# A hybrid retention and attention trunk on one core: score matmuls of one height, projections grouped, output halves sharing their accumulators

## The chip, the cores and the metric

The kernel runs on one core of a Trainium2 chip. The metric is the device time of one execution in microseconds, the median of the runs shown. TensorE (PE; its weight loads are PEld), VectorE (DVE), ScalarE (ACT), GpSimd (POOL) and SyncE (SP) each work through an instruction stream of their own and wait for one another by semaphores.

## The reference, cut to what matters

512 tokens of width 1024 pass through two layers. Each layer is: half a SwiGLU feed-forward, a token mixer, half a SwiGLU feed-forward, a gated extra embedding; an RMS norm stands ahead of each. The mixer of layer 0 is retention (4 heads), that of layer 1 is attention with a forget gate (16 heads of 64), which is where most of the change lies:

```
q, k, v, fz = split(h @ w_in)                         # 16 heads of 64, fz: 16 logits a token
c = cumsum(log_sigmoid(fz + b_f))                     # over the tokens
logits = (q @ k.T) * scale + c[query] - c[key]        # causal
o = softmax(logits) @ v
return o.reshape(S, 1024) @ w_out
```

## The kernel before, in words

Activations are kept with features on the partitions and the 512 tokens along the free dimension (`h[m]`, eight blocks). Each fp32 operand is split into a rounded part (hi) and a rest (lo), and a product is three matmuls (`mm3`, L301 to L303: hi with hi, hi with lo, lo with hi). Weights come through SP's queue into `wraw` (4 buffers); ACT makes the hi part (L79), and DVE or POOL, whichever `W.low` names, the lo part (L80), into `w` (3 buffers). `W.plan` is the order of all weights; `W.take` insists on that order and prepares two ahead. A PSUM accumulator is one of 8 banks (`bank()`). The order on PE is the order of the program text; on the other engines a planner orders the instructions by priority and by estimated times. A norm's scale per token is made in two steps: `n.columns` (L426, then a chain of small DVE and ACT operations) gives it with tokens on partitions, `n.rows` (L445 transposes, L439) spreads it over all partitions. Projections don't need it; their evictions do.

**Retention** (L679) projects q and k of head 0, calls `n.columns` and `n.rows` and spreads the variance (L732 to L734), then projects v (`v_part`, L673 to L675, 96 matmuls). At its end `out_both` (L634) applies the output weights of the last two heads into shared accumulators, four blocks ahead of the last head's results.

**The forgetting attention** (L824) works on pairs of heads, `p` = 0 to 7, with 64 partitions for each head of the pair. First comes the gate: the projection `fz`, columns, rows, and a chain of some thirty DVE and ACT operations on 16 partitions (L835 to L872) to the cumulated gates, which go to DRAM (L873) and come back broadcast, one row for each head (L941), then masked by POOL (L942). `k_part` (L889) and `q_part` (L906) project one pair each (24 matmuls of 512 columns), and split: `khi[e]` holds head e's hi keys on both halves of the partitions, `klo` the lo keys of both heads, each on its own half; `q[e]` holds the hi queries on head e's half and the lo queries on the other. `scores` (L923) then needs two matmuls for each query block i, of (i+1)*128 columns:

```
nc.tensor.matmul(at[i], q[e][own[e], i * P : w], klo[own[e], :w], start=True, stop=False)   # L933: 64 partitions
nc.tensor.matmul(at[i], q[e][:, i * P : w], khi[e][:, :w], start=False, stop=True)          # L936: 128 partitions
```

into three banks for each head, and writes the softmax for DVE and ACT (L955 to L967). `turn` (L972) transposes a head's probabilities (10 transposes, L982, three banks) and splits them (L292, L293); `attend` (L988) multiplies them with v (8 matmuls, L995 and L996) and adds two halves (L998, L999). The order that PE follows in a round of the loop (L1014) is: k projection of pair p+1; attend for head 0 of pair p-1; turn head 0 of pair p; q projection; attend for head 1; turn head 1; scores of pair p+1. Round 0 has no attend and turns both heads after the q projection; round 4 also projects the second half of v (96 matmuls). In round 7 and after, `out_part` (L620) applies the output weights of heads 0 to 7 (96 matmuls in all, each block added to `h[m]`, L630) between the same steps; after the last attend it applies those of heads 8 to 15 (96 matmuls), again with one addition for each block, and prepares the next feed-forward's input block by block (`nxt.block`). `open_ffn(3)` has DVE form weight sums at the same time. The feed-forward that follows starts with `product` (L478), which needs all eight blocks.

Of the kernel before, what the change touches and what calls it, by code (L numbers as in the profile page):

```python
# [17 lines left out]
P = 128  # L18
S = 512
# [154 lines left out]
def trunk(ctx, tc, a):  # L174
# [77 lines left out]
    W.plan += fox_o[0] + fox_o[1]  # L252
# [381 lines left out]
    def out_both(parts, nxt, early, between, late):  # L634


        banks = {}

        def add(i, m, first, last):
            srcs, yhi, ylo = parts[i]  # L640
            j = m % 2
            if (i, m // 2) not in banks:
                banks[i, m // 2] = W.take(srcs[m // 2])
            wh, wl = banks[i, m // 2]
            o = banks.setdefault(m, None)
            if o is None:
                o = banks[m] = bank()
            for k in range(4):
                ks = slice((4 * j + k) * P, (4 * j + k + 1) * P)
                mm3(o, wh[:, ks], wl[:, ks], yhi[k], ylo[k], first and k == 0, last and k == 3)  # L650

        for m in early:
            add(0, m, True, False)
        between()
        for m in early + late:
            if m in late:
                add(0, m, True, False)
            add(1, m, False, True)
            nc.vector.tensor_tensor(out=h[m], in0=banks[m], in1=h[m], op=ALU.add)
            nxt.block(m)  # L660
# [18 lines left out]
    def retention(n, nxt):  # L679
        with ExitStack() as pools:  # L680
            stack = []
            pool = pools.enter_context(tc.tile_pool(name="ret", bufs=1, reuse_waits="tile"))
# [43 lines left out]
            for hd in range(RH):  # L726
                dk = pool.tile([P, S], F32, name="decay", bufs=2)
                nc.sync.dma_start(out=dk, in_=a["decay"][hd])
                if hd == 0:
# [3 lines left out]
                    n.rows()  # L733
                    nc.scalar.mul(epsv, spread(n.v), EPS)  # L734
# [7 lines left out]
                vs = v_part(ret_v[hd], n)  # L742
                v = []
# [71 lines left out]
            def between():  # L815
                outputs()
                pools.close()
                stack.append(open_ffn(1))

            out_both([(ret_o[RH - 2], *before), (ret_o[RH - 1], *y)], nxt, [0, 1, 2, 3], between, [4, 5, 6, 7])  # L820
        return stack[0]


    def forgetting(n, nxt):  # L824
        H = 64
        with tc.tile_pool(name="fox", bufs=1, reuse_waits="tile") as pool:
# [4 lines left out]
            (fz,) = proj([a["fox_f"]], n)  # L831
            n.columns()
            n.rows()
# [54 lines left out]

            def k_part(p):  # L889

                (o,) = proj([fox_qk[p][0]], n)
                t1 = temp()
                nc.vector.tensor_tensor(out=t1, in0=o, in1=n.r, op=ALU.mult)
                klo = pool.tile([P, S], F32R, name="klo")
                khi = []
                for e in range(2):
# [7 lines left out]
                return khi, klo  # L904

            def q_part(p):  # L906

                (o,) = proj([fox_qk[p][1]], n)
# [14 lines left out]
            def scores(p, q, k):  # L923

                khi, klo = k
# [87 lines left out]
            old = None  # L1013
            for p in range(8):  # L1014
                last = p == 7
                if last:
                    out_part(fox_o[0], yhi[0:4], ylo[0:4], None, range(1))
                else:
                    k = k_part(p + 1)
                if old:  # L1020
                    y = temp()
                    attend(p - 1, 0, v, old[0], y)
                    new = [turn(0, sm[0])]
                if last:
                    out_part(fox_o[0], yhi[0:4], ylo[0:4], None, range(1, 2))
                else:
                    q = q_part(p + 1)
# [8 lines left out]
                if not last:  # L1036
                    sm = scores(p + 1, q, k)
# [250 lines left out]
```

## Time and profile before

| | |
|---|---|
| median of 3 runs | 2306.04 us (2305.58 to 2314.34) |
| the profiled execution | 2314.51 us, of which the span is 2312.6 us |
| mean granted TensorE clock | 0.966 of full speed |
| PE busy | 2192.7 us (95%) |
| DVE busy | 1537.3 us (66%) |
| ACT busy, POOL busy | 1210.0 us (52%), 460.0 us (20%) |
| chain that ended last | PE 73%, DVE 10%, ACT 7%, DMA 6% |

The span is read from left to right in 40 slices. Retention fills about 376 to 793 us, the forgetting attention about 1565 to 1864 us, and the feed-forwards the rest. "Idle before" is the time for which an engine stood still ahead of an instruction, with the instruction that ended it.

### The profile page before, as it was taken

The numbers are of one execution on the slowest core, as the hardware profiler recorded it, in microseconds if no ns is written. First come the engines' busy times: TensorE is split into PE (matmuls) and PEld (weight loads), VectorE is DVE, ScalarE is ACT, GpSimd is POOL, SyncE is SP. The second block draws the span as 40 slices with busy tenths as digits, with TensorE's granted clock in tenths as the row PEclk, the third lists the DMA queues.
The fourth block names the chain that finished last, engine by engine and source line by source line (L and its number), as shares of the span: only waits on it lengthen the run. The fifth ranks groups of instructions, "written<-read, shape, count | busy, mean of one in ns | idle before, by whom it ended". The sixth has DMA issues, their size and how long they took to land.

```text
span 2312.6 us, 34447 instructions
## 1 busy us (share of the span) xinstructions
PE 2192.7 (95%) x13417; PEld 1955.9 (85%) x13417; DVE 1537.3 (66%) x2813; ACT 1210.0 (52%) x2022; POOL 460.0 (20%) x347
## 2 busy tenths in 40 slices
PE   7998999999999899999989899999999989999998
PEld 7898987888888798989879899897777779898977
DVE  8676766264453976767687676776775787676774
ACT  7464554333233673646466455455564576363653
POOL 0010103344443010101101011014222211010144
PEclk9999999999999999999999999999889989999998
DMA  6474652222322464646345465543222246464631
GB/s 192 119 179 123 150 143 93 75 96 73 100 82 73 119 163 129 156 131 157 105 127 121 130 150 152 145 115 101 65 64 82 69 108 163 117 160 132 147 109 37
DMA packets 87907, 274.94 MB, mean 119 GB/s; under 512 B 9648, under 2 KB 13232, under 8 KB 87744
## 3 DMA queue, kind: packets, MB, share of 16 engines
q1 hardware_dynamic: 63328, 209.78, 27.7%
q0 software_dynamic: 23184, 61.88, 16.0%
q8 instruction: 105, 1.72, 0.3%
q10 hardware_dynamic: 1232, 1.09, 0.1%
q14 instruction: 58, 0.48, 0.1%
HBM read 270.58 MB, written 2.13 MB: 118 GB/s over the span
## 4 chain that ended last, share of the span: by engine, by line
PE 73%; DVE 10%; ACT 7%; DMA 6%; issue 2%; POOL 0%; SPq 0%; ACTq 0%; DVEq 0%; POOLq 0%
PE bank L478 24%; PE bank L303 13%; PE bank L301 13%; PE bank L302 13%; DMA wraw<-in_ffn_w_in 5%; DVE sums L141 2%; PE bank L673 2%; PE bank L674 2%; PE bank L675 2%; ACT w L117 1%; ACT s L79 1%; DVE w L80 1%; ACT w L118 1%; PE bank L936 1%; PE bank L933 1%
## 5 line engine op out<-in xcount | busy, mean ns | idle before, releaser
L79 ACT CAST w<-wraw 128x1024 fp32r<-128x1024 f32 (+1 forms) x224 | 226.7, 1020 | 443.3 <-PE bank L303 286.4
L80 DVE TENSOR_TENSOR s<-sums,s 128x512 fp32r<-128x512 f32 x344 | 232.6, 687 | 116.0 <-ACT s L79 115.5
L79 ACT CAST s<-sums 128x512 fp32r<-128x512 f32 x344 | 208.2, 617 | 190.4 <-DVE sums L141 139.1
L303 PE MATMUL bank<-unit_a,w 128*128 128x512 f32 (+1 forms) x752 | 292.3, 389 | 4.4 <-DVE w L80 2.7
L301 PE MATMUL bank<-unit_a,w 128*128 128x512 f32 (+1 forms) x752 | 293.4, 390 | 2.4 <-ACT w L79 2.0
L302 PE MATMUL bank<-unit_a,w 128*128 128x512 f32 (+1 forms) x752 | 291.8, 388 | 0.8 <-DVE unit_a L293 0.8
L301 PE MATMUL bank<-unit_d,w 128*128 128x512 f32 (+1 forms) x744 | 287.4, 386 | 3.6 <-ACT w L79 1.8
L302 PE MATMUL bank<-unit_d,w 128*128 128x512 f32 (+1 forms) x744 | 285.6, 384 | 5.1 <-DVE unit_d L296 3.9
L303 PE MATMUL bank<-unit_d,w 128*128 128x512 f32 (+1 forms) x744 | 285.0, 383 | 2.7 <-DVE w L80 2.7
L80 POOL TENSOR_TENSOR w<-wraw,w 128x1024 fp32r<-128x1024 f32 x90 | 220.1, 2449 | 323.5 <-ACT w L79 312.5
L478 PE MATMUL bank<-unit_b,s 128*128 128x256 f32 x952 | 205.1, 282 | 0.0
L119 POOL DMA_DIRECT2D a<-in_ffn_w_in x86 | 75.2, 874 | 612.2 <-ACT a L118 540.3
L478 PE MATMUL bank<-unit_d,s 128*128 128x256 f32 x1188 | 194.3, 281 | 0.0
L119 POOL DMA_DIRECT2D w<-in_ffn_w_in x75 | 65.6, 875 | 645.2 <-ACT w L118 518.2
L478 PE MATMUL bank<-unit_a,s 128*128 128x256 f32 x1314 | 186.6, 279 | 2.9 <-ACT unit_a L361 2.4
L302 PEld LDWEIGHTS bank<-unit_d,w 128*128 128x128 f32 x744 | 145.1, 195 | 32.2 <-DVE unit_d L296 4.1
L141 DVE TENSOR_TENSOR sums<-wraw 128x512 f32<-128x512 f32 x172 | 118.0, 688 | 81.6 <-DMA wraw<-in_ffn_w_in 80.3
L301 PEld LDWEIGHTS bank<-unit_d,w 128*128 128x128 f32 x744 | 145.3, 195 | 31.5 <-ACT w L79 3.5
L478 PE MATMUL bank<-unit_b,w 128*128 128x256 f32 x774 | 147.7, 291 | 25.2 <-ACT tmp L529 24.6
L303 PEld LDWEIGHTS bank<-unit_a,w 128*128 128x128 f32 x752 | 141.5, 188 | 35.5 <-DVE w L80 4.5
L569 DVE SCALAR_TENSOR_TENSOR tmp<-bank,rows 128x512 f32<-128x512 f32 x96 | 66.0, 689 | 158.2 <-PE bank L303 154.5
L478 PEld LDWEIGHTS bank<-unit_a,s 128*128 128x128 f32 x1314 | 167.7, 190 | 3.5 <-ACT unit_a L361 2.6
(266 smaller groups left out, 4942.9 us busy)
## 6 DMA issues: line engine op xcount, KB each, us to landing
wraw<-in_ffn_w_in SPq DMA_DIRECT2D x174, 512.0 KB, 4.6
w<-in_ffn_w_in POOLq DMA_DIRECT2D x75, 512.0 KB, 5.6
wraw<-in_ffn_w_out SPq DMA_DIRECT2D x64, 512.0 KB, 5.0
a<-in_ffn_w_in POOLq DMA_DIRECT2D x86, 256.0 KB, 6.5
wraw<-in_ffn_w_out SPq DMA_DIRECT2D x32, 384.0 KB, 4.3
wraw<-in_ret_qk SPq DMA_DIRECT2D x16, 512.0 KB, 3.4
wraw<-in_ret_v SPq DMA_DIRECT2D x16, 512.0 KB, 3.7
wraw<-in_ret_g SPq DMA_DIRECT2D x16, 512.0 KB, 3.5
```

The costliest lines, as they stand in the source:

```text
L79: self.nc.scalar.copy(hi, raw)
L80: self.low.tensor_tensor(out=lo, in0=raw, in1=hi.bitcast(F32), op=ALU.subtract)
L119: self.nc.gpsimd.dma_start(out=lo, in_=src, accum_op=ALU.add)
L141: add = lambda o, p, q: nc.vector.tensor_tensor(out=o, in0=p, in1=q, op=ALU.add)
L301: nc.tensor.matmul(out, wh, xh, start=first, stop=False)
L302: nc.tensor.matmul(out, wh, xl, start=False, stop=False)
L303: nc.tensor.matmul(out, wl, xh, start=False, stop=last)
L478: add = lambda w, x, start, stop: nc.tensor.matmul(out, w, x, start=start, stop=stop, skip_group_check=True)
L569: nc.vector.scalar_tensor_tensor(out=t1, in0=o, scalar=-0.5, in1=n.r, op0=ALU.mult, op1=ALU.mult)
L673: nc.tensor.matmul(os[t], xh, wh[:, js], start=k == 0, stop=False)
L674: nc.tensor.matmul(os[t], xh, wl[:, js], start=False, stop=False)
L675: nc.tensor.matmul(os[t], xl, wh[:, js], start=False, stop=k == KB - 1)
```

## The change

It has five parts. (1) In retention's head 0 the rows and the variance are spread after `v_part` instead of before it. (2) In the attention the k projection of pair 0 stands ahead of the columns and its q projection ahead of the rows. (3) The lo keys get a tile for each head, `klo0` and `klo1`, zeroed once by POOL on the half that isn't written, so that the L933 matmul can run on all 128 partitions with the same stationary operand as L936. (4) A round is now: k and q projections, both attends, both turns, scores. (5) The output halves share accumulators: `out_both` becomes the class `OutBoth`, used by retention in the same order as before, and by the attention with six blocks of heads 0 to 7 begun ahead of the last attend (two ahead of the attends of round 7, two ahead of its turns, two after them) and the last two blocks at the end; the order of the output weights in the plan follows.

```diff
-    W.plan += fox_o[0] + fox_o[1]
+    W.plan += fox_o[0][0:3] + fox_o[1][0:3] + [fox_o[0][3], fox_o[1][3]]
...
+    class OutBoth:
...
+        def add(self, i, m):
...
+                mm3(self.banks[m], wh[:, ks], wl[:, ks], yhi[k], ylo[k], i == 0 and k == 0, i == 1 and k == 3)
+        def first(self, ms):
+            for m in ms:
+                self.banks[m] = bank()
+                self.add(0, m)
+        def rest(self):
+            for m in range(KB):
+                if m not in self.banks:
+                    self.first([m])
+                self.add(1, m)
+                nc.vector.tensor_tensor(out=h[m], in0=self.banks[m], in1=h[m], op=ALU.add)
+                self.nxt.block(m)
...
     def retention(n, nxt):
...
                     n.columns()
-                    n.rows()
-                    nc.scalar.mul(epsv, spread(n.v), EPS)
...
                 vs = v_part(ret_v[hd], n)
+                if hd == 0:
+                    n.rows()
+                    nc.scalar.mul(epsv, spread(n.v), EPS)
...
     def forgetting(n, nxt):
...
             (fz,) = proj([a["fox_f"]], n)
+            begun = [proj([s], n)[0] for s in fox_qk[0][0:1]]
             n.columns()
+            begun += proj(fox_qk[0][1:2], n)
             n.rows()
...
+            lows = []
+            for e in range(2):
+                lows.append(pool.tile([P, S], F32R, name=f"klo{e}"))
+                nc.gpsimd.memset(lows[e].bitcast(F32), 0.0)
...
-                        out=klo[own[e]], in0=t1[own[e]], in1=kh[own[e]].bitcast(F32), op=ALU.subtract
+                        out=lows[e][own[e]], in0=t1[own[e]], in1=kh[own[e]].bitcast(F32), op=ALU.subtract
...
-                            nc.tensor.matmul(at[i], q[e][own[e], i * P : w], klo[own[e], :w], start=True, stop=False)
+                            nc.tensor.matmul(at[i], q[e][:, i * P : w], lows[e][:, :w], start=True, stop=False)
...
+            both = OutBoth([(fox_o[0], yhi, ylo), (fox_o[1], [], [])], nxt)
             for p in range(8):
-                last = p == 7
-                if last:
-                    out_part(fox_o[0], yhi[0:4], ylo[0:4], None, range(1))
+                if p < 7:
+                    k, q = k_part(p + 1), q_part(p + 1)
                 else:
-                    k = k_part(p + 1)
+                    both.first((0, 1))
                 if old:
                     y = temp()
-                    attend(p - 1, 0, v, old[0], y)
-                    new = [turn(0, sm[0])]
...
+                    for e in range(2):
+                        attend(p - 1, e, v, old[e], y)
                     split_y(y)
...
                 if p == 4:
                     v = v_block(1)
-                new.append(turn(1, sm[1]))
-                if not last:
+                if p == 7:
+                    both.first((2, 3))
+                old = [turn(e, sm[e]) for e in range(2)]
+                if p < 7:
                     sm = scores(p + 1, q, k)
-                old = new
-            out_part(fox_o[0], yhi[0:4], ylo[0:4], None, range(2, 4))
+            both.first((4, 5))
             y = temp()
             for e in range(2):
                 attend(7, e, v, old[e], y)
             split_y(y)
+            both.parts[1] = fox_o[1], yhi[4:8], ylo[4:8]
             W.low = nc.vector
         stack = open_ffn(3)
-        out_part(fox_o[1], yhi[4:8], ylo[4:8], nxt)
+        both.rest()
```

## Rows read from the trace of the kernel before

**Rows 1.** The page: the granted TensorE clock in the span's 40 slices, in tenths.

```profile
PEclk9999999999999999999999999999889989999998
```

**Rows 2.** Busy time by stretch: stretch, length, then PE, PEld, DVE, ACT and POOL busy with their instructions, the granted clock, DMA share, GB/s. The first is from the first score matmul of pair 1 to that of pair 7.

```profile
1629.16:1802.07 172.91, 165.12 (x697) 128.42 (x697) 119.87 (x412) 96.98 (x212) 46.68 (x29) 0.86 0.21 67
1656.00:1682.00 26.00, 24.69 (x100) 18.93 (x100) 19.06 (x67) 14.54 (x33) 5.84 (x5) 0.80 0.20 61
1755.02:1775.72 20.70, 20.60 (x101) 16.27 (x100) 17.60 (x69) 15.17 (x37) 7.20 (x5) 1.00 0.22 76
```

**Rows 3.** The timeline of PE where a round's scores begin and where the next round begins: start, duration, line, operation, tiles, shapes, count, and in brackets the idle time before.

```profile
1657.74 0.62 PE L936 MATMUL bank<-khi,q 128*128 128x256 f32 x2 [1.31 <-DVE q L917]
...
1663.74 0.63 PE L301 MATMUL bank<-unit_d,w 128*128 128x512 f32 x1
1664.17 0.63 PE L302 MATMUL bank<-unit_d,w 128*128 128x512 f32 x1
```

**Rows 4.** The timeline of PE at full clock: scores of one pair without a wait, to the projection after them; one head's turn and the projection after it; two attends in a row, first matmul and the one after the last. The last row is of the attend's line: count, and shortest, median and longest weight load in ns.

```profile
1755.02 0.62 PE L933 MATMUL bank<-klo,q 64*128 64x256 f32 x2
...
1759.85 0.39 PE L301 MATMUL bank<-unit_d,w 128*128 128x512 f32 x1
...
1646.62 1.28 PE L982 MATMUL bank<-ident,p 128*128 128x128 f32 x10
1647.66 0.47 PE L301 MATMUL bank<-unit_d,w 128*128 128x512 f32 x1
...
1837.47 0.40 PE L995 MATMUL bank<-thi,unit_b 128*128 128x512 f32 x1
...
1839.96 0.45 PE L301 MATMUL bank<-unit_a,w 128*128 128x512 f32 x1
...
L995 PEld LDWEIGHTS bank<-thi,unit_b x64: 186/188/193, 1645.2 to 1839.7; 128*128 128x128 f32 x64
```

**Rows 5.** The timeline of PE: round 0 from its two turns on, and the first scores of pair 7.

```profile
1626.62 2.35 PE L982 MATMUL bank<-ident,p 128*128 128x128 f32 x20
1629.16 0.61 PE L933 MATMUL bank<-klo,q 64*128 64x256 f32 x2 [0.19 <-ACT q L916]
1630.95 0.62 PE L936 MATMUL bank<-khi,q 128*128 128x256 f32 x2 [1.19 <-DVE q L917]
1632.39 0.47 PE L933 MATMUL bank<-klo,q 64*128 64x128 f32 x1 [0.82 <-DVE tlo L293]
...
1802.07 0.61 PE L933 MATMUL bank<-klo,q 64*128 64x256 f32 x2 [0.15 <-ACT q L916]
```

**Rows 6.** The timeline of DVE around the scores of the same round as in rows 3.

```profile
1655.80 2.60 DVE L917 TENSOR_TENSOR q<-tmp,q 64x512 fp32r<-64x512 f32 x2 [0.69 <-ACT q L916]
1658.44 0.68 DVE L999 TENSOR_TENSOR tmp<-bank,tmp 64x512 f32<-64x512 f32 x1
1659.15 1.29 DVE L293 TENSOR_TENSOR tlo<-bank,thi 128x512 fp32r<-128x512 f32 x2
1660.36 0.68 DVE L293 TENSOR_TENSOR unit_a<-tmp,unit_a 128x512 fp32r<-128x512 f32 x1
1660.95 0.42 DVE L293 TENSOR_TENSOR tlo<-bank,thi 128x256 fp32r<-128x256 f32 x1
```

**Rows 7.** The timeline around the columns and rows of retention's head 0: PE, the two weight splits on POOL, and the first use of the rows on DVE.

```profile
399.83 0.95 PE L426 MATMUL bank<-ones_r,tmp 128*128 128x2 f32 x8
400.58 5.10 POOL L80 TENSOR_TENSOR w<-wraw,w 128x1024 fp32r<-128x1024 f32 x2 [7.88 <-issue]
...
407.93 1.12 PE L445 MATMUL bank<-ident,cols 128*128 128x128 f32 x4 [7.15 <-DVE cols L454]
...
409.55 0.78 PE L673 MATMUL bank<-w,unit_a 128*128 128x512 f32 x1
...
413.08 0.40 PE L675 MATMUL bank<-w,unit_a 128*128 128x512 f32 x1
...
442.53 0.69 DVE L772 TENSOR_TENSOR tmp<-bank,rows 128x512 f32<-128x512 f32 x1 [2.92 <-PE bank L303]
```

**Rows 8.** The timeline at the start of the attention: PE at the gate's projection (first and last of 24 matmuls), the rows and the first matmul of v; then POOL's mask for pair 0 and the first softmax instruction of DVE.

```profile
1565.46 0.39 PE L301 MATMUL bank<-unit_d,w 128*128 128x512 f32 x1
...
1570.67 0.39 PE L303 MATMUL bank<-unit_d,w 128*128 128x512 f32 x1
...
1575.60 1.12 PE L445 MATMUL bank<-ident,cols 128*128 128x128 f32 x4 [2.11 <-DVE cols L454]
...
1589.26 0.39 PE L673 MATMUL bank<-w,unit_d 128*128 128x512 f32 x1
...
1608.19 0.64 POOL L942 TENSOR_SCALAR_AFFINE_SELECT unit_c<-unit_c 128x512 f32<-128x512 f32 x1 [4.08 <-DMA unit_c<-cdram]
...
1612.08 0.29 DVE L955 CUSTOM_DVE_ANT_0 p<-bank,unit_c 128x128 f32<-128x128 f32 x1 [0.49 <-PE bank L936]
```

**Rows 9.** The timeline of PE: the first matmul that needs the last split result of the attention, the feed-forward's wait after the output weights, and the same two waits after retention.

```profile
1842.63 0.50 PE L301 MATMUL bank<-unit_a,w 128*128 128x512 f32 x1 [0.39 <-ACT unit_a L292]
...
1871.82 1.04 PE L478 MATMUL bank<-unit_d,w 128*128 128x256 f32 x2 [7.43 <-ACT unit_d L369]
...
795.17 0.39 PE L478 MATMUL bank<-unit_a,w 128*128 128x256 f32 x1 [1.21 <-ACT unit_a L369]
796.34 0.39 PE L478 MATMUL bank<-unit_a,w 128*128 128x256 f32 x1 [0.79 <-DVE unit_a L370]
```

More of the change, by code (lines that the diff above doesn't have):

```diff
@@ L632, in out_part, with __init__ @@
                     nxt.block(m)
[L634 to L647, printed above, removed]
-            for k in range(4):
[L649 to L660, printed above, removed]
+    class OutBoth:
+        def __init__(self, parts, nxt):
+            self.parts, self.nxt, self.ws, self.banks = parts, nxt, {}, {}
+        def add(self, i, m):
+            srcs, yhi, ylo = self.parts[i]
+            if (i, m // 2) not in self.ws:
+                self.ws[i, m // 2] = W.take(srcs[m // 2])
+            wh, wl = self.ws[i, m // 2]
+            for k in range(4):
+                ks = slice((4 * (m % 2) + k) * P, (4 * (m % 2) + k + 1) * P)
+                mm3(self.banks[m], wh[:, ks], wl[:, ks], yhi[k], ylo[k], i == 0 and k == 0, i == 1 and k == 3)
[10 more added lines that the diff above has]
+                self.nxt.block(m)
     def v_part(srcs, n):
@@ L679, in retention @@
     def retention(n, nxt):
-        with ExitStack() as pools:
-            stack = []
-            pool = pools.enter_context(tc.tile_pool(name="ret", bufs=1, reuse_waits="tile"))
+        with tc.tile_pool(name="ret", bufs=1, reuse_waits="tile") as pool:
             W.low = nc.gpsimd
@@ L813, in retention @@
             W.low = nc.vector
[L815 to L821, printed above, removed]
+            both = OutBoth([(ret_o[RH - 2], *before), (ret_o[RH - 1], *y)], nxt)
+            both.first(range(4))
+            outputs()
+        stack = open_ffn(1)
+        both.rest()
+        return stack
     def forgetting(n, nxt):
@@ L1013, in forgetting @@
             old = None
+            both = OutBoth([(fox_o[0], yhi, ylo), (fox_o[1], [], [])], nxt)
             for p in range(8):
-                last = p == 7
-                if last:
-                    out_part(fox_o[0], yhi[0:4], ylo[0:4], None, range(1))
+                if p < 7:
+                    k, q = k_part(p + 1), q_part(p + 1)
                 else:
-                    k = k_part(p + 1)
+                    both.first((0, 1))
                 if old:
                     y = temp()
-                    attend(p - 1, 0, v, old[0], y)
-                    new = [turn(0, sm[0])]
[L1024 to L1027, printed above, removed]
-                if old:
-                    attend(p - 1, 1, v, old[1], y)
+                    for e in range(2):
+                        attend(p - 1, e, v, old[e], y)
                     split_y(y)
-                else:
-                    new = [turn(0, sm[0])]
                 if p == 4:
                     v = v_block(1)
-                new.append(turn(1, sm[1]))
-                if not last:
+                if p == 7:
+                    both.first((2, 3))
+                old = [turn(e, sm[e]) for e in range(2)]
+                if p < 7:
                     sm = scores(p + 1, q, k)
-                old = new
-            out_part(fox_o[0], yhi[0:4], ylo[0:4], None, range(2, 4))
+            both.first((4, 5))
             y = temp()
@@ L1043, in forgetting @@
             split_y(y)
+            both.parts[1] = fox_o[1], yhi[4:8], ylo[4:8]
             W.low = nc.vector
         stack = open_ffn(3)
-        out_part(fox_o[1], yhi[4:8], ylo[4:8], nxt)
+        both.rest()
         return stack
```

9 lines of the change are left out of this document (4 added, 5 removed).

## The prediction, written before the change ran

> **What bounds the kernel now.** The granted clock over the slices first: it is full nearly everywhere and falls to 0.8 in the slices of the forgetting attention [rows 1]. The same view by stretch then gives the stage: from the scores of pair 1 to those of pair 7, 172.9 us, PE is busy for 165.1 and DVE for only 119.9, so PE bounds it, but at a mean clock of 0.86 [rows 2]. Clock counts between 1 (2.4 GHz) and 0.5 (1.2 GHz), so (1 - 0.86) x 172.9 = 24 us of full speed are missing there. The timeline of PE says what went before a fall: a wait of 1.3 us for the lo queries, scores at wide spacing, and then the next projection issues every 0.43 us [rows 3], against (1570.67 - 1565.46)/23 = 0.2265 us at full clock [rows 8]. The pair whose scores had no wait ran at 1.00, its whole round in 20.7 us [rows 2, 4].
>
> I take the second v projection out at 96 x 0.2265 = 21.7 us, and six rounds are left: (172.9 - 21.7)/6 = **25.2 us a round**. At full clock and without waits a round is: k and q projections 48 x 0.2265 = 10.9; two attends 1839.96 - 1837.47 = 2.5; two turns 2 x (1647.66 - 1646.62) = 2.1; scores 1759.85 - 1755.02 = 4.8 [rows 4, 8]. That is 20.3; with 24/6 = 4.0 for the clock and about 1.3 of waits it is 25.6, which is the measured round within 0.4.
>
> **Scores on 128 partitions.** The 16 score matmuls of a pair have the same column counts as the 16 of two attends (128 to 512, each twice for each head), yet take 4.8 us against 2.5 [rows 4]; they differ in that 64 and 128 partitions alternate. With all on 128 I price them as the attends: 4.8 - 2.5 = **2.3 us less a round**, ends 0 and 2.3. The lo split costs DVE the same as before; the two memsets run on POOL once, ahead of everything that needs them, and with POOL busy for 46.7 of 172.9 us [rows 2] I cost them at nothing (without that cover, one mask's 0.64 each [rows 8]).
>
> Here a rule of the Trainium skill speaks against it: "TensorE: Matmul & The Clock Gate", Part 3 (packing small matmuls), says that weight loads overlap with matmuls in flight only when their row groups differ. By it the new scores would gain nothing; the attends, all on the same rows, contradict it.
>
> **The new order of a round.** PE's floor is 10.9 + 2.5 + 2.1 + 2.5 = 18.0 us. DVE was busy for 19.1 of a 26 us stretch and 17.6 of the fast round's 20.7 [rows 2], so from the other side a round can hardly be under 18 either. The queries now have attends and turns, 4.6 us, between their projection and the scores. In round 0, which turns both heads right after the q projection, the waits were 0.19 + 1.19 for the queries, only 2.3 us of turns lying between, and 0.82 for banks of the second head [rows 5]; 2.5 us of attends more cover the queries' 1.4. The bank wait should grow: eight banks are full after the turns (two attends, six transposes) and scores need six, freed by two additions of 0.68 us and the split results behind them [rows 6], which formerly ran half under the q projection. I take 1.5 us of waits a round, near round 0's 0.82; ends 0 and 6.8. For the clock I take a fall in one round of three, 4.0/3 = 1.3 us, since dense scores and a shorter wait leave less of what preceded the falls, but two turns now stand together; ends 0 and 5.2, which is (1 - 0.80) x 26 [rows 2]. Sum: 18.0 + 1.5 + 1.3 = **20.8 us, 4.4 less; six rounds 26 us**.
>
> **Retention's rows, later.** PE waits 7.15 us for the columns, spends 1.6 us on transposes, and begins v at 409.55 on half clock: eight matmuls until 413.08 [rows 7], 3.5 us instead of 8 x 0.2265 = 1.8. Moved, v starts at 399.83 + 0.95 = 400.78, and eight transposes at 0.104 [rows 4] come after it: 409.55 - 400.78 - 0.83 + 1.7 = **9.6 us less**, ends 7 and 9.6. The columns' chain is hidden by the 21.7 us of v; the first use of the rows is at 442.53. POOL's next weight pair starts at 400.58 and its first half, due 24 x 0.2265 = 5.4 us into v, is done after 2.6 [rows 7].
>
> **The attention's start.** k then runs from 1570.9, q ends at about 1582.7 with the columns' 2.11 us wait under it, and v starts at 1583.2 instead of 1589.26: 6.1 us earlier on PE [rows 8]. But the rows, on which the gate's chain hangs, come at 1582.7 instead of 1575.60, 7.1 later. With everything behind it on DVE, ACT, SP's queue (the store and the broadcast loads) and POOL's, the mask of pair 0 moves from 1608.19 to 1615.3, and the softmax that began at 1612.08 [rows 8] can't finish masking until then: 3.3 us later. PE has two projections in between, and then the turn waits. Between 6.1 gained and 3.3 lost I take **0**.
>
> **Output halves.** From the scores of pair 7 to the last attend's split results the old PE needs 1842.63 - 1802.07 = 40.6 us [rows 5, 9]. The new one: scores 2.5, 72 matmuls instead of 96 at 0.2265 = 16.3, four attends 5.0, turns 2.1, the split's waits of some 1.2, and bank waits, since held accumulators leave turns fewer banks, 1.5: 28.6, so 12 less. After that the old tail is 1871.82 - 1842.63 = 29.2 us, of which 7.43 is a wait for DVE-bound block preparation [rows 9]; the new one has 120 matmuls, 27.2 us, and then waits as after retention, whose output already works this way, 1.21 + 0.79 = 2.0 [rows 9]: 29.2, plus one more weight split, on DVE, and unknown sums order, 2. Eight additions to `h` go; they lay ahead of the last attend, where PE waited for no DVE work but the 1.2 us above, so I cost them at nothing (at most 8 x 0.68 = 5.4). **10 us less**, ends 3 and 12. Retention's own end keeps its sequence: 0.
>
> **Sum.** 9.6 + 26 + 0 + 10 = 46 us. The profiled execution took 2314.5, which is 8.5 over the median of 2306.0; 2314.5 - 46 = 2268.5, and taken to the median **2260 us**.
>
> **Rivals.**
> *Rounds near the floor* (0.18): waits of 0.3 and no falls, 18.3 a round, six save 41; the attention's start keeps its 6: 41 + 9.6 + 6 + 10 = 67, so 2239. For it: the fast round without a fall, less 2.3, is 18.4. Against: DVE would have to be busy nearly throughout.
>
> *The clock still falls in every round* (0.19): two turns in a row, then a bank wait. A round is 18.0 + 1.5 + 4.0 = 23.5; six save 10, the whole 30, so 2276. For it: round 0 has just this order, and its waits add to 2.2 us [rows 5]. Against: its scores were still wide.
> The same page's Part 4 (PE-mode transpose) says that transposes don't count as PE activity as matmuls do; by it this rival would be the forecast. No row here separates transposes from the wait behind them.
>
> *128 partitions bring nothing* (0.04): if each score matmul had to expose its weight load of 0.188 us, 16 x 0.188 on top of the 2.1 us of columns would be 5.1, and a round 18.0 + 2.6 + 1.5 + 1.3 = 23.4; six save 11, the whole 31, so 2275. This is what Part 3's rule would make of it; the attends' loads of the same length stand against it [rows 4].
>
> *No change* (0.10): bank waits and falls together bring the rounds back to 24 or 25 and the gate's chain costs its 3.3; only retention's 9.6 and some of the output stay, so 2295 to 2303.
>
> *Slower* (0.06): banks decide. If nothing of the queries' 2.6, two additions, six splits (3.4) and the result's split 0.68, 8.0 us in all [rows 6], runs before the turns end, the second head's scores wait 8.0 less the first head's 1.2, and the longer gap costs the worst clock: 18.0 + 6.8 + 5.2 = 30.0, +29 over six rounds; with the gate's 3.3, none of the output's gain and retention's -9.6 it is +23, so 2329. It decides from a round of 28 us on. Against: DVE was idle for 7 us in 26 [rows 2].
>
> **How the numbers follow.** The forecast has 0.43. About 0.5% (11.5 us) is what a measurement of this kernel can tell from no change. Forecast, fast rounds, falling clock and useless padding are all faster by more: 0.84. The range, 2238 to 2290, reaches from the fast rivals through the falling clock to the edge of no change; it leaves out the slower case and most of no change, with a little at the fast end.
>
> **What would show it.** Right: score matmuls of 128 partitions, 2.5 us a pair where no wait lies between; rounds of 20 to 22 us; a mean clock in the stage of 0.92 or more; no wait of L445 in retention; first matmul of the feed-forward after about 2 us instead of 7.43. Wrong: PE waits ahead of scores or turns of over 3 us, a clock of 0.86 as before, or DVE as the engine that PE waits for in each round.

## The result, and the profile after

The kernel after takes **2283.98 us** (median of 4 runs, 2281.49 to 2286.48) against 2308.25 before (2305.58 to 2314.34, on the same chip): ratio 0.9891, 95% interval 0.9866 to 0.9917, 24 us less. Forecast were 46 less, to 2260 us. The profiled execution after took 2286.48 us, with a span of 2284.5; the spans differ by 28.1 us, since the execution of before that was profiled lay higher over its median than that of after.

Where the 28.1 us are, from the first matmul of each stretch to the first of the next, in us ("untouched": the change edits nothing there):

| stretch | before | after | difference | forecast |
|---|---|---|---|---|
| start to retention's first column sums (untouched) | 399.8 | 394.8 | -5.0 | 0 |
| from there to the projection behind v and the spread | 33.2 | 23.5 | -9.7 | -9.6 |
| rest of retention, its output, and the next feed-forward's first products | 371.3 | 371.0 | -0.3 | 0 |
| feed-forwards and per-layer part (untouched) | 728.4 | 731.8 | +3.4 | 0 |
| last 144 output matmuls of a feed-forward (32.7 in both), gate's projection, to the scores of pair 1 | 96.4 | 97.7 | +1.3 | 0 |
| scores of pair 1 to scores of pair 7 | 172.9 | 155.6 | -17.3 | -26 |
| scores of pair 7 to the end of the feed-forward's first wait | 69.8 | 68.1 | -1.6 | -10 |
| everything behind (untouched) | 441 | 442 | +1 | 0 |

Untouched stretches differ by up to 5 us between these two executions, and by more over all: in the 14 kernels profiled in this study, the first one took 390.7 to 399.8. A difference of a few us in one stage has to be read in that stage.

**The rounds.** By stretch (length; busy time of PE, PE's loads, DVE, ACT and POOL, with counts; granted clock; DMA share and GB/s) the kernel after shows two rounds, the whole stage that answers to [rows 2], and the stretch behind it to the end of the wait:

```profile
1640.61:1663.56 22.95, 20.59 (x100) 17.24 (x100) 20.35 (x68) 14.70 (x33) 6.20 (x4) 0.93 0.23 69
1663.56:1685.10 21.54, 19.16 (x101) 15.96 (x101) 20.25 (x68) 14.71 (x33) 6.27 (x4) 1.00 0.23 74
1618.86:1774.50 155.64, 143.37 (x696) 119.67 (x696) 124.55 (x410) 94.58 (x208) 46.60 (x28) 0.95 0.24 77
1774.50:1842.64 68.14, 59.09 (x266) 48.27 (x266) 53.74 (x133) 42.86 (x83) 8.22 (x6) 0.91 0.28 76
```

The mean clock went from 0.86 to 0.95, and a round lasts 21 to 24 us (22.3 in the mean, without the 21.8 of the second v projection). PE is idle for 1.6 to 2.4 us of a round, 2.0 in the mean ((155.6 - 143.4)/6). What it waits for in a round with 2.4 stands in PE's timeline (start, length, idle time before and its releaser) at the place that answers to [rows 3]:

```profile
1659.70 2.37 PE L987 MATMUL bank<-ident,p 128*128 128x128 f32 x20
1663.56 0.39 PE L938 MATMUL bank<-klo,q 128*128 128x256 f32 x1 [1.49 <-DVE tmp L1004]
1664.28 0.50 PE L938 MATMUL bank<-klo,q 128*128 128x512 f32 x1 [0.33 <-DVE tmp L1004]
...
1666.53 0.50 PE L938 MATMUL bank<-klo,q 128*128 128x512 f32 x1 [0.55 <-DVE tlo L293]
...
1667.81 0.42 PE L301 MATMUL bank<-unit_d,w 128*128 128x512 f32 x1
```

The wait for the lo queries is gone; PE now waits for banks: 1.49 + 0.33 us until the additions of the two attends (L1004) free theirs, then 0.55 for a split result of the turns. The next view, DVE's timeline at this place, shows what the additions were behind:

```profile
1659.78 3.02 DVE L922 TENSOR_TENSOR q<-tmp,q 64x512 fp32r<-64x512 f32 x2 [0.74 <-ACT q L921]
1662.82 1.40 DVE L1004 TENSOR_TENSOR tmp<-bank,tmp 64x512 f32<-64x512 f32 x2
```

Two lo splits of 64x512 last 3.02 us. POOL's timeline of the same stretch has the reason, a weight split that ends 1.27 us ahead of them:

```profile
1659.15 2.38 POOL L80 TENSOR_TENSOR w<-wraw,w 128x1024 fp32r<-128x1024 f32 x1 [2.82 <-ACT w L79]
```

This stands under every round: the six pairs last 2.95 to 3.04 us, one split up to 2.32. A DVE instruction that waits for POOL counts as busy here, so DVE's waits name nothing; it shows only in the length. The groups of the stage (count, busy time, mean ns) have the same form twice, first with both operands in SBUF, then with one in PSUM:

```profile
L922 DVE TENSOR_TENSOR q<-tmp,q 64x512 fp32r<-64x512 f32 x14 | 20.4, 1454 | 5.3 <-ACT q L921 5.1
...
L1004 DVE TENSOR_TENSOR tmp<-bank,tmp 64x512 f32<-64x512 f32 x12 | 8.2, 683 | 0.4
```

It was there before too. The same group in the kernel before, over 1629 to 1802 us:

```profile
L917 DVE TENSOR_TENSOR q<-tmp,q 64x512 fp32r<-64x512 f32 x12 | 15.2, 1266 | 4.5 <-ACT q L916 4.3
```

**Retention's start** (answers to [rows 7]): v follows the column sums at once, and the spread comes after v with no wait.

```profile
394.83 0.95 PE L426 MATMUL bank<-ones_r,tmp 128*128 128x2 f32 x8
395.64 0.49 PE L673 MATMUL bank<-w,unit_a 128*128 128x512 f32 x1
...
417.54 0.60 PE L445 MATMUL bank<-ident,cols 128*128 128x128 f32 x4
417.98 0.60 PE L445 MATMUL bank<-ident,cv 128*128 128x128 f32 x4
418.33 0.47 PE L301 MATMUL bank<-unit_b 128*128 128x512 f32 x1
```

**The output's end** (answers to [rows 9]): the 7.43 us of wait ahead of the feed-forward's second group are 6.91 now.

```profile
1834.87 0.64 PE L478 MATMUL bank<-unit_b,w 128*128 128x256 f32 x4
1835.34 0.40 PE L478 MATMUL bank<-unit_d,w 128*128 128x256 f32 x2
1842.64 1.04 PE L478 MATMUL bank<-unit_d,w 128*128 128x256 f32 x2 [6.91 <-ACT unit_d L369]
```

DVE at that place is busy throughout, first by stretch, then in its timeline: the last two additions to `h` (L659) start at 1838.89, behind the sums for the next weights (L141, L80), though PE was through with both banks and began the feed-forward at 1834.87.

```profile
1810.39:1842.19 31.80, 25.35 (x115) 20.90 (x113) 31.08 (x59) 26.33 (x46) 3.02 (x4) 0.93 0.42 99
```

```profile
1838.29 0.69 DVE L141 TENSOR_TENSOR sums<-wraw 128x512 f32<-128x512 f32 x1
1838.89 1.29 DVE L659 TENSOR_TENSOR hall<-bank,hall 128x512 f32<-128x512 f32 x2
```

### The profile page after: what moved, and what is told of

Same layout as the page of the kernel before. It is cut to its first block, busy times and chain, and to the rows that moved or that the text cites. A ratio compares the mean times of both kernels' runs of the same rounds, so it can differ in the third digit from the quotient of the medians.

```text
span 2284.5 us, 34462 instructions
## 1 busy us (share of the span) xinstructions
PE 2162.6 (95%) x13417; PEld 1942.9 (85%) x13417; DVE 1538.1 (67%) x2806; ACT 1208.1 (53%) x2022; POOL 458.2 (20%) x348
## 3 DMA queue, kind: packets, MB, share of 16 engines
HBM read 270.58 MB, written 2.13 MB: 119 GB/s over the span
## 4 chain that ended last, share of the span: by engine, by line
PE 69%; DVE 12%; ACT 8%; DMA 7%; issue 3%; POOL 0%; SPq 0%; ACTq 0%; DVEq 0%; POOLq 0%
PE bank L478 24%; PE bank L303 13%; PE bank L301 13%; PE bank L302 13%; DMA wraw<-in_ffn_w_in 7%; DVE sums L141 2%; PE bank L673 2%; PE bank L674 2%; PE bank L675 2%; ACT w L117 1%; ACT s L79 1%; ACT w L118 1%; DVE w L80 1%; DVE s L80 1%; ACT a L118 1%
## 5 line engine op out<-in xcount | busy, mean ns | idle before, releaser
L80 DVE TENSOR_TENSOR s<-sums,s 128x512 fp32r<-128x512 f32 x344 | 232.6, 686 | 116.4 <-ACT s L79 116.2
L301 PE MATMUL bank<-unit_d,w 128*128 128x512 f32 (+1 forms) x744 | 282.9, 380 | 3.6 <-ACT w L79 1.8
L302 PE MATMUL bank<-unit_d,w 128*128 128x512 f32 (+1 forms) x744 | 281.5, 378 | 5.0 <-DVE unit_d L296 3.9
L303 PE MATMUL bank<-unit_d,w 128*128 128x512 f32 (+1 forms) x744 | 280.6, 377 | 2.7 <-DVE w L80 2.7
L80 POOL TENSOR_TENSOR w<-wraw,w 128x1024 fp32r<-128x1024 f32 x89 | 217.3, 2444 | 285.5 <-ACT w L79 273.2
L141 DVE TENSOR_TENSOR sums<-wraw 128x512 f32<-128x512 f32 x172 | 118.0, 688 | 86.5 <-DMA wraw<-in_ffn_w_in 85.8
L80 DVE TENSOR_TENSOR w<-wraw,w 128x1024 fp32r<-128x1024 f32 (+1 forms) x135 | 157.6, 1173 | 18.9 <-ACT w L79 18.7
L301 PEld LDWEIGHTS bank<-unit_d,w 128*128 128x128 f32 x744 | 142.5, 192 | 31.9 <-ACT w L79 3.5
```

Of the source, the lines that this page charges most:

```text
L80: self.low.tensor_tensor(out=lo, in0=raw, in1=hi.bitcast(F32), op=ALU.subtract)
L141: add = lambda o, p, q: nc.vector.tensor_tensor(out=o, in0=p, in1=q, op=ALU.add)
L301: nc.tensor.matmul(out, wh, xh, start=first, stop=False)
L302: nc.tensor.matmul(out, wh, xl, start=False, stop=False)
L303: nc.tensor.matmul(out, wl, xh, start=False, stop=last)
```

## The experiments

Ratios are to the kernel before on the same chip. "Stage" is the stretch from the scores of pair 1 to those of pair 7, "end" that from the scores of pair 7 to the feed-forward's first matmul, before the wait for DVE. The last kernel leaves out work (its section below).

| kernel | median us | ratio, 95% interval | stage us | clock | end us |
|---|---|---|---|---|---|
| before | 2308.25 | | 172.9 | 0.86 | 61.5 |
| after | 2283.98 | 0.9891, 0.9866 to 0.9917 | 155.6 | 0.95 | 60.4 |
| pad_alone | 2279.89 | 0.9860, 0.9836 to 0.9883 | 146.9 | 0.99 | 56.8 |
| order_alone | 2316.07 | 1.0024, 1.0010 to 1.0039 | 179.2 | 0.86 | 62.2 |
| rows_alone | 2300.59 | 0.9958, 0.9943 to 0.9973 | 173.2 | 0.86 | 61.5 |
| start_alone | 2307.17 | 0.9987, 0.9972 to 1.0002 | 172.1 | 0.87 | 61.5 |
| pad_order | 2290.07 | 0.9909, 0.9889 to 0.9929 | 156.0 | 0.95 | 58.3 |
| three_parts | 2267.18 | 0.9809, 0.9793 to 0.9825 | 148.0 | 0.98 | 55.4 |
| old_rounds | 2262.56 | 0.9792, 0.9775 to 0.9808 | 149.9 | 0.97 | 56.0 |
| three_q_psum | 2263.33 | 0.9792, 0.9760 to 0.9825 | 143.4 | 1.00 | 56.3 |
| old_q_psum | 2260.93 | 0.9787, 0.9765 to 0.9810 | 143.4 | 1.00 | 56.9 |
| after_q_psum | 2256.32 | 0.9775, 0.9756 to 0.9793 | 141.4 | 1.00 | 57.4 |
| before_q_psum | 2288.49 | 0.9902, 0.9869 to 0.9935 | 156.6 | 0.92 | 57.2 |
| after_less_dve | 2272.21 | 0.9840, 0.9826 to 0.9855 | 157.3 | 0.92 | 57.8 |

### Each part alone

**pad_alone**: the padding of the change's diff (two cleared `klo` tiles, whole-height operands) and nothing else.

```diff
-nc.tensor.matmul(at[i], q[e][own[e], i * P : w], klo[own[e], :w], start=True, stop=False)
+nc.tensor.matmul(at[i], q[e][:, i * P : w], lows[e][:, :w], start=True, stop=False)
```

> The kernel before with the score matmuls of all eight pairs on 128 partitions and nothing else of the change. Stage read: from the scores of pair 1 to those of pair 7, 172.9 us before, 155.6 after the whole change. Theory A (the matmuls themselves carry the gain): scores fall from 4.8 to about 2.5 us a pair, the wait for the lo queries stays at some 1.3 us or grows by 0.3, because now the first matmul needs them too, and the clock still falls behind it: stage 158 to 161, whole kernel 12 to 15 us less. Rival B (dense scores also end the clock's falls): stage 145 to 150 at a clock over 0.95, 23 to 28 us less. Rival C (128 partitions bring nothing without the new order, since the earlier need for the lo queries costs what they save): stage 168 or more, at most 5 us less.

It takes 31 us off, more than the whole change. Rival B is right in the stage, 146.9 us at a clock of 0.99, and 3 us short in the whole: 4.6 more are in the end, where the clock rose from 0.94 to 0.97. By stretch, then in PE's timeline of one round:

```profile
1667.87:1688.55 20.68, 18.55 (x101) 15.86 (x101) 19.16 (x68) 14.90 (x34) 6.61 (x4) 1.00 0.25 77
1624.43:1771.36 146.93, 135.17 (x696) 114.66 (x697) 119.55 (x412) 97.76 (x213) 47.14 (x28) 0.99 0.25 79
```

```profile
1664.46 1.28 PE L986 MATMUL bank<-ident,p 128*128 128x128 f32 x10
1667.87 0.59 PE L937 MATMUL bank<-klo,q 128*128 128x256 f32 x2 [2.13 <-DVE q L921]
...
1668.64 0.22 PE L937 MATMUL bank<-klo,q 128*128 128x128 f32 x1
1668.70 0.27 PE L940 MATMUL bank<-khi,q 128*128 128x128 f32 x1
...
1670.62 0.41 PE L301 MATMUL bank<-unit_d,w 128*128 128x512 f32 x1
```

The 16 matmuls take 1670.62 - 1667.87 = 2.75 us instead of 4.83 [rows 4]. The kernel before has, for the two matmuls of 128 columns:

```profile
1756.16 0.29 PE L933 MATMUL bank<-klo,q 64*128 64x128 f32 x1
1756.38 0.33 PE L936 MATMUL bank<-khi,q 128*128 128x128 f32 x1
```

From one start to the next these are 0.22 us where the heights differ and 0.06 where both are 128. Over the pair, 1.5 of the 2.1 us lie in the eleven steps from one height to the other, the rest in steps between equal ones. The wait for the lo queries is longer than before, 2.1 us a round, and still the clock falls in one round of the stage only.

**order_alone**: the kernel before with the new order of pairs 0 to 6, in short:

```diff
-k = k_part(p + 1); attend(0); turn(0); q = q_part(p + 1); attend(1); split_y; turn(1)
+k, q = k_part(p + 1), q_part(p + 1); attend(0); attend(1); split_y; turn(0); turn(1)
```

> The kernel before with only the order of a round changed: both projections of the next pair, two attends, two turns, scores; scores still alternate 64 and 128 partitions, retention, the attention's start and the output are as before. Theory A: the wait for the lo queries goes and waits for banks of about 2.4 us a round, as in the kernel after, take its place, while the clock keeps falling behind the wide scores: stage from the scores of pair 1 to those of pair 7 between 172 and 180 us, whole kernel 0 to 7 us more. Rival B (the order is what keeps the clock up): clock of the stage at 0.93 or more, stage 160 to 165, 8 to 13 us less.

Theory A: 5 us slower, stage 6 us longer. Over the scores of pairs 1 to 7 there are 9.1 us of waits for the additions (10 times, at most 1.5) where 7.6 us for the lo queries had been.

**rows_alone** and **start_alone**: those parts of the change's diff, in short.

```diff
+vs = v_part(ret_v[hd], n)
+if hd == 0: n.rows(); nc.scalar.mul(epsv, spread(n.v), EPS)      (rows_alone)
+begun = k of pair 0; n.columns(); begun += q of pair 0; n.rows()   (start_alone)
```

> The kernel before with only retention's spread of the token scales moved behind the first v projection. Theory A: from the first columns matmul to the end of v and the spread 23.5 us instead of 33.3 and nothing given back later in retention, whole kernel 9 to 10 us less. Rival: the store, the broadcast and the epsilon come too late for the first head and 3 us or more return as a wait of DVE or PE before the first gate, so 6 us less or fewer.

> The kernel before with only the attention's start changed: projection of pair 0's k, columns, projection of its q, then the spread of the token scales. Stage read: from the gate's projection to the scores of pair 1, 96.4 us before and 97.7 after the whole change. Theory A (the later gate chain gives back on DVE what PE gains): scores of pair 0 wait 3 us or more for the banks that the split of v holds, stage 96 to 99, whole kernel between 1 less and 3 more. Rival B (the move itself gains the 6 us of PE time, and the loss in the whole change came from another part, the padded scores or the new order of round 0): stage 89 to 92, 4 to 7 us less.

Retention's part gains what was forecast: 23.5 us for that stretch, 10.6 in all. The start's stage took 94.8 us, between the two theories, and PE's wait for the banks that the split of v holds was 1.9 us and not 3 (in after it is 3.4); 4 us less in all, with an interval that takes in 1. The stage of 96.4 us begins 32.7 us ahead of the gate's projection, as in the table above. Over all profiled kernels it took 96.4 to 99.8 in the old form (6 kernels, mean 98.2) and 94.8 to 98.5 in the new one (8 kernels, mean 97.2). About 1 us, which no total here can show.

### What the order does to the padded scores

**pad_order**: pad_alone and order_alone together.

> The kernel before with two parts of the change: scores on 128 partitions, and the new order of a round (both projections, two attends, two turns, scores). With the scores alone the stage from the scores of pair 1 to those of pair 7 took 146.9 us at a clock of 0.99. Theory A (the new order trades one wait of 2.1 us for the lo queries against several for banks, 1.5 + 0.3 + 0.6, and they come behind 20 transposes in a row, so that the clock falls again): stage 154 to 158 at a clock of 0.94 to 0.96, 7 to 10 us slower than the scores alone. Rival (the order is harmless on 128 partitions, and the whole change lost its 9 us in this stage to its other parts): stage 145 to 149.

**three_parts**: pad_alone, rows_alone and start_alone together.

> The kernel before with scores on 128 partitions, retention's rows later and the attention's start changed; the order of a round and the output stay as before. Theory A (the parts add): retention's start 23.5 us, rounds from pair 1 to pair 7 147 us, from the scores of pair 7 to the feed-forward 57 us; 38 to 43 us less than before, some 15 less than the whole change. Rival (what one part saves, another gives back): 33 us less or fewer.

**old_rounds**: the whole change with only the order of pairs 0 to 6 undone.

> The whole change with one thing undone: pairs 0 to 6 run in the old order of a round; the last pair and the output in halves stay as in the change. Theory A (the new order costs, and the output halves gain little because DVE sets the end of that stretch): rounds 147 us, from the scores of pair 7 to the feed-forward's first matmul 56 to 60 us with 6 to 7.5 us of wait behind it, whole kernel 36 to 43 us less than before. Rival B (the halves gain the predicted 10 us once the rounds are in order): that stretch 47 to 50 us, whole kernel 46 us less or more.

Theory A twice, and a third time in the stretches: falls of the clock spread the stage by some 3 us, and old_rounds took 47 us off where theory A had 36 to 43 and rival B 46 or more. Its end is theory A's, 56.0 us. The order takes 9.1 us back in the stage (156.0 against 146.9); the three other parts add up to 42 us; undoing the order in the whole change gives another 21 to 23 us (0.9792 against 0.9891), some 6 of them in the stage and 4 in the end; of the rest 5 us stand behind the feed-forward's first wait, where no edit reaches. And the output in halves is worth nothing that can be seen here: old_rounds and three_parts differ in it and in little else, and need 56.0 and 55.4 us to the feed-forward, with a wait of 6.7 and 7.4 behind. By stretch, the end of after, three_parts and old_rounds:

```profile
1774.50:1834.87 60.37, 58.23 (x261) 47.61 (x262) 46.69 (x121) 38.10 (x76) 6.55 (x4) 0.94 0.20 57
1765.15:1820.57 55.42, 54.25 (x260) 45.23 (x261) 46.83 (x120) 35.84 (x70) 9.86 (x6) 1.00 0.30 86
1766.26:1822.25 55.99, 54.78 (x260) 45.25 (x261) 45.57 (x119) 37.13 (x73) 6.55 (x4) 1.00 0.22 66
```

The 4 us by which after is longer are its clock, 0.94 against 1.00.

### What the bank wait is made of

**three_q_psum** (on three_parts), **after_q_psum** (on after), **old_q_psum** (on old_rounds) and **before_q_psum** (on before) all have one edit in `q_part`; the lo split then reads the bank and one SBUF operand:

```diff
-t1 = temp()
+t1 = o
 nc.vector.scalar_tensor_tensor(out=t1, in0=o, scalar=H ** -0.5, in1=n.r, op0=ALU.mult, op1=ALU.mult)
```

> As the kernel with the three parts (scores, rows, start), with one edit: the scaled queries are written back into their PSUM bank instead of an SBUF tile, so that the lo split of the queries reads one operand from PSUM. In the kernel after, the 14 lo splits of the stage take 1.45 us in the mean, against 0.69 where POOL runs nothing, and each pair of them ends 1.3 us after POOL's weight split of 2.4 us; splits that read PSUM show 0.68 us throughout. Theory A (DVE waits for POOL when both operands are in SBUF): 0.69 us each, PE's wait for the lo queries falls from 2.1 us to about 0.8 a round, rounds of 19.4 us, stage 139 to 141, 6 to 9 us less than the three parts. Rival B (they are long because they write the other half of the partitions): 1.3 us each as before, stage 146 to 148.

The splits take 688 ns, as theory A has it, though they still write the other half of the partitions; the group of the stage, answering to the L922 of after:

```profile
L924 DVE TENSOR_TENSOR q<-bank,q 64x512 fp32r<-64x512 f32 x14 | 9.6, 688 | 5.2 <-ACT q L923 5.0
```

The wait falls from 2.13 to 0.89 us, but the stage only to 143.4: the second split now stands behind an addition and a turn's split on DVE, and the second head's scores wait 0.54 for it. That is 4.6 us less than three_parts where theory A had 6 to 9, part of it by the clock (0.98 to 1.00), and the total is not told apart from three_parts.

> The whole change with one edit: the scaled queries stay in their PSUM bank, so that their lo splits don't wait for POOL. In the kernel after, two lo splits take 3.0 us behind POOL's weight split, the two additions that free the banks of the attends end 1.4 us after them, and PE waits 1.5 us for the first. Theory A (POOL's weight split is what makes the bank wait of the new order): splits of 0.69 us, the wait ahead of the scores falls from 1.5 to 0.5 us or less, stage from the scores of pair 1 to those of pair 7 148 to 150 us with the falls of the clock as they were, 146 or less if the falls go too. Rival B (the additions and the split results themselves fill DVE at this place, whoever holds the queries): wait of 1.2 us or more, stage 153 to 156.

Theory A, with the falls of the clock gone too: 141.4 us. PE's and then DVE's timeline of one round, same place as in the kernel after:

```profile
1650.02 2.37 PE L987 MATMUL bank<-ident,p 128*128 128x128 f32 x20
1652.31 0.39 PE L938 MATMUL bank<-klo,q 128*128 128x256 f32 x1
1653.03 0.50 PE L938 MATMUL bank<-klo,q 128*128 128x512 f32 x1 [0.33 <-DVE tmp L1004]
...
1655.28 0.50 PE L938 MATMUL bank<-klo,q 128*128 128x512 f32 x1 [0.55 <-DVE tlo L293]
...
1656.56 0.41 PE L301 MATMUL bank<-unit_d,w 128*128 128x512 f32 x1
```

```profile
1650.13 0.68 DVE L922 TENSOR_TENSOR q<-bank,q 64x512 fp32r<-64x512 f32 x1 [0.70 <-ACT q L921]
1650.85 0.68 DVE L1004 TENSOR_TENSOR tmp<-bank,tmp 64x512 f32<-64x512 f32 x1
1651.56 0.69 DVE L922 TENSOR_TENSOR q<-bank,q 64x512 fp32r<-64x512 f32 x1
1652.29 0.68 DVE L1004 TENSOR_TENSOR tmp<-bank,tmp 64x512 f32<-64x512 f32 x1
```

The wait of 1.49 us is gone and the clock does not fall in the whole stage:

```profile
1632.37:1652.31 19.94, 19.07 (x101) 15.96 (x101) 18.69 (x68) 14.64 (x34) 6.30 (x4) 1.00 0.24 79
1612.98:1754.37 141.39, 136.41 (x697) 113.71 (x697) 115.48 (x410) 94.57 (x210) 47.55 (x29) 1.00 0.25 83
```

This kernel has the lowest median here, 53 us below before and some 27 below after (0.9775 against 0.9891); 14.2 of these are in the stage and 3.0 in the end. Most of the other 10 are in stretches that the edit doesn't touch (6.5 behind the feed-forward's first wait), so they can't be put down to it.

> The whole change with the old order of a round for pairs 0 to 6 and the queries kept in PSUM. Theory A (both repairs add): rounds of 20.4 us as with the three parts and this edit, stage 143 to 145 us, whole kernel 45 to 52 us less than before. Rival (the two overlap, since both remove the same wait): 40 us less or fewer.

Theory A: 49 us less. Its stage is 2.0 us longer than that of after_q_psum, so in the stage the new order is the better one once the splits don't wait for POOL; in the totals the two are not told apart (intervals 0.9765 to 0.9810 and 0.9756 to 0.9793).

> The kernel before with one edit: the scaled queries stay in their PSUM bank, so that their lo splits don't wait for POOL; score matmuls still alternate 64 and 128 partitions. PE's wait of 1.3 us for the lo queries should go or fall to 0.3. Theory A (widely spaced scores alone are enough for the clock to fall, as each of these pairs shows it behind them): clock of the stage from the scores of pair 1 to those of pair 7 0.84 to 0.89, stage 165 to 172 us, 1 to 8 us less than before. Rival B (the clock falls only where a wait comes on top): clock 0.95 or more, stage 148 to 154, about 20 us less.

Neither theory in the stage, 156.6 us at a clock of 0.92; the total, 21 us less, is as B has it, with 4 us of them in the end. No wait for the queries is left, and the clock still falls in four of the stretches between two scores:

```profile
1625.66:1651.92 26.26, 25.13 (x101) 19.16 (x101) 18.54 (x69) 14.85 (x35) 6.05 (x5) 0.81 0.18 61
...
1673.93:1694.24 20.31, 20.31 (x101) 16.20 (x101) 18.37 (x68) 14.84 (x34) 6.05 (x5) 1.00 0.26 79
```

### What bounds the output's end

**after_less_dve**: the kernel after without seven additions on DVE in the norm behind the output, in short:

```diff
-else: add.tensor_tensor(out=self.acc[:, ts_], in0=self.acc[:, ts_], in1=sq, op=ALU.add)
+elif not self.bare: add.tensor_tensor(...)      # bare for this one norm
```

> The whole change, but the sum of squares of the norm behind the attention's output takes block 0 alone: the seven additions of 0.69 us on DVE, which nothing of PE's work ahead of the feed-forward reads, are left out. Read: PE's wait behind the first matmuls of the feed-forward, 6.9 us in the kernel after. Theory A (DVE's queue sets the end of this stretch: additions to the residual, blocks and weight sums, 27 us of work): the wait falls by 3 to 5 us, to 2 to 4. Rival B (the two adds come late because ACT waits for the weights' DMA at this place): wait 6 us or more, as before.

The waits of PE in this stretch (total, times, longest):

```profile
PE bank L478 <- DVE unit_d L370: 0.8, 1, 0.8
PE bank L478 <- ACT unit_d L369: 0.8, 1, 0.8
```

6.9 us fell to 1.6: theory A, a little beyond its 2 to 4. Seven additions are 7 x 0.69 = 4.8 us, and the wait shrank by 5.3.

## Why the prediction was right in its direction and 22 us short

**Retention's rows**: 9.6 forecast, 9.7 measured, in the change and alone. **Attention's start**: 0 forecast, +1.3 in the pair of profiles, about -1 over all kernels. PE comes to the scores of pair 0 6.2 us earlier, as forecast, and gives it back, but not on the path that was named (mask, softmax, then the turn; 3.3 us, 3.2 by its rows): PE waits 3.4 and 0.9 us within these scores for banks that the split of v holds, and DVE comes to that split (1596.61) right behind the last addition of the gate's chain (1596.02).

**Rounds**: 20.8 us forecast, 22.3 measured. The term "scores 4.8 to 2.5 us" held (2.75 in pad_alone). That pad_alone took just the 26 us off the stage that were forecast for all parts together is chance: six times 2.08 us are 12.5, and the rest came with the clock, which stayed up although the wait for the queries grew to 2.1 us. The new order, from which the prediction expected no loss, took 9.1 us of it back (pad_order). The mean round is 19.1 us of work at full clock, 2.0 of waits and 1.2 of clock, where the prediction had 18.0, 1.5 and 1.3:
- *The floor of 18.0* is 19.07, by the round of after_q_psum at full clock: 10.9 and 2.5 as taken, but turns of 2.29 instead of 2.1, and scores of 1656.56 - 1652.31 = 4.25 us, less 0.33 + 0.55 of idle time 3.37. That is 0.62 more than where they run without a stop: each of the two stops costs 0.3 us beside its idle time (in three_q_psum, with one stop of 0.54, they take 3.59 - 0.54 = 3.05).
- *The bank waits of 1.5* were 2.0 in the mean and 1.49 + 0.33 + 0.55 = 2.4 in three of the six rounds. The step counted the additions and splits behind the turns by their own lengths, 0.68 us, and left out what DVE does just ahead of them. Those two lo splits of the queries took 3.0 us instead of 1.4 because POOL was splitting weights. That the queries' wait would be covered by attends and turns was right, but their splits stayed in DVE's queue, ahead of what PE waits for next. The row was there: [rows 6] has 2.60 us for two such splits beside 0.68 for an addition of the same size, and the prediction took it for work ("the queries' 2.6").
- *The clock, 1.3*, is about right: PE is busy for (143.4 - 21.75)/6 = 20.3 us a round, 1.2 more than at full clock. It falls in four of the six rounds.

One of the prediction's own signs of being wrong came true: DVE is the engine that PE waits for in each round.

Here the Trainium skill has the rule that the prediction should have weighed: "SBUF — State Buffer", section "Who interferes with whom", says that a DVE instruction with two SBUF inputs contends with a GpSimd instruction that reads SBUF, and calls the port pair that they share an exclusive lock. The trace agrees: 1454 ns in the mean with both inputs in SBUF, 688 with one in PSUM; in each of the six pairs of splits the first lasts until 0.55 to 0.6 us after POOL's weight split has ended, and the second takes 0.69.

The rule of the Trainium skill that the prediction weighed, weight loads overlapping only where row groups differ, is not borne out: scores on the same 128 rows take 2.75 us, nearly the attends' 2.49 and less than their sixteen weight loads one after another (16 x 0.189 = 3.0). What fits the 4.8 us is what the Trainium skill says in "TensorEngine Tiling (Array Packing)", section "Key Properties": a change of tiling mode drains TensorE. Scores that alternated 64 and 128 rows changed it for each group of them, and most of the difference lies in those steps; but no run has scores on 64 rows alone, so this is argued and not shown.

**Output halves**: 10 forecast, 1.6 measured, 0 by old_rounds against three_parts. The step that failed is "and then waits as after retention, 2.0": the 7.43 us didn't go, because DVE and not PE sets the end of that stretch, 31.1 us busy of 31.8, and without 4.8 us of DVE's work the wait is 1.6. The prediction itself called that wait bound by DVE, and then took it as gone. A second term went with it: the 28.6 us from the scores of pair 7 to the last attend's split results are 34.6 in after. The step set a new stretch at full clock against an old one at 0.92, and after has 0.90 there (old_rounds at 1.00: 30.2). The halves themselves take no matmul away, so PE does not reach the feed-forward earlier by them: 56.0 us against 55.4.

**Rivals**: "the clock still falls in every round" came nearest in its size (2276), but it falls in four of six, each time by less than was assumed, and the bank waits carry more of the loss (2.0 us a round against 1.2). "Slower, by banks" had the right place, with a price far too high: at most 2.4 us of waits instead of 6.8. "128 partitions bring nothing" is refuted by pad_alone.

**Sum**: 45.6 (rounded to 46) - 28.1 = 17.5 us were missing between the two spans: 8.7 in the rounds, 8.4 in the output, 1.3 at the start, less 1.0 that retention and the untouched stretches happened to save. The 24 us of the medians are less than 28.1 since the profiled execution of before lay 6 us over its median and that of after 2.5.

What makes the clock fall is not settled. It falls with alternating rows and no wait for the queries (0.92), now and then with dense scores behind a wait of 2.1 us or of 1.5 us (0.92 to 0.99), and in no round from the scores of pair 1 on in the three kernels with dense scores and single waits under 1 us, 20 transposes in a row or 10. In their round 0, with a wait of 4.5 us or more, it is 0.86 or 0.87. That transposes in a row are enough to pull it down, as the rival could have had it with the Trainium skill's "TensorE: Matmul & The Clock Gate", Part 4, is not seen: after_q_psum has all 20 at a clock of 1.00.

## What to carry to other kernels

Price the parts of a change by where each engine's queue stands, not by PE's order alone: a wait that is covered still leaves its work in front of the next thing that PE needs. A DVE instruction whose length varied from 0.69 to 2.3 us at one shape was waiting for another engine here; look at what POOL does at that moment before trusting its mean. And where a wait ends on an engine that is busy throughout the stretch, count that engine's work before expecting anything from moving PE's, which brought nothing here. And compare two stretches at one clock: a term priced at full clock against a row at 0.92 promises a gain that the edit may not bring.

## What the runs showed of the hardware that had not been expected

Sixteen score matmuls take 4.8 us where 64 and 128 rows alternate and 2.75 where all have 128, for the same columns, and with that alone the stage's clock rose from 0.86 to 0.99. Two DVE splits of 64x512 with both inputs in SBUF took 3.0 us under a POOL split of 2.4 us, 1.4 with one input in PSUM.
